# Spreading the latent norm factor of an MLA layer over the partitions: four transposes in place of a DRAM write and read

## The chip, the core and the metric

The kernel runs on one core of one Trainium2 chip. The metric is the device time of one execution in microseconds, as the median over runs. A core has a matrix engine (TensorE, PE in the profile; PEld is its weight load), a vector engine (VectorE, DVE), a scalar engine (ScalarE, ACT), a general engine (GpSimd, POOL) and a sync engine (SyncE, SP), which here issues the DMA transfers. Each engine works through its own queue in order and waits on semaphores for the others. TensorE writes to the accumulator memory PSUM; the working memory is SBUF, with 128 partitions.

## What is computed

A two-layer encoder trunk over 1024 positions of width 1024, batch 1, in float32. Layer 0 is differential attention. Layer 1 is multi-head latent attention, and the change lies at its start:

```python
def _rmsnorm(x, g):
    xf = x.astype(jnp.float32)
    y = xf * lax.rsqrt(jnp.mean(xf * xf, axis=-1, keepdims=True) + RMS_EPS)
    return (y * g.astype(jnp.float32)).astype(x.dtype)

def _mla(h, positions, w_in, q_a_norm_g, w_q_b, kv_a_norm_g, w_kv_b, w_out):
    proj = h @ w_in
    q_a, c_kv, k_pe, z = jnp.split(proj, [384, 640, 704], axis=-1)
    q = (_rmsnorm(q_a, q_a_norm_g) @ w_q_b).reshape(b, s, 8, 192)
    ...
    kv = (_rmsnorm(c_kv, kv_a_norm_g) @ w_kv_b).reshape(b, s, 8, 256)
    k_nope, v = kv[..., :128], kv[..., 128:]
    ...
    return o @ w_out
```

The two latents are the query latent (384 wide) and the key/value latent (256 wide). Each position of a latent is divided by its root mean square over the latent's width and multiplied by a gain per column.

## The kernel before

The kernel keeps activations transposed: partitions hold columns, the free dimension holds positions. Positions come in two halves of 512. Every float32 product is made of three matmuls on a high and a low part of each operand (`mm3`, lines 186 to 188). A high part is a rounding copy on ACT, the low part a subtraction on DVE or GpSimd.

The instructions of each engine are put in order by a planner that uses costs of its own, so the order on the chip isn't always that of the code; only instructions marked with `in_turn`, `issue_after` or `keep_in_program_order` are tied down.

Layer 1 begins with the rotary part of the key, the first gate tiles, and then the latents. `lora` (lines 1397 to 1447) returns the consumer for one latent. The key/value latent has n = 2 tiles of 128 columns for each half, the query latent n = 3. For each tile `put` copies the accumulator to SBUF (L1404) and squares it on ACT (L1408, L1411); DVE adds the squares up (L1412). When the last tile of a half is there, a list called `norms` takes over. `run_norms` (L1373) is called at fixed places of the code, and at each it runs what stands in the list at that moment, which may append the next step. The steps are:

- `norm` (L1419): four small matmuls with a column of ones (L1422) sum the squares over the partitions. The result is a 128x4 tile: position 128 j + p of the half is at partition p, column j. DVE takes the mean and adds epsilon (L1424), GpSimd raises to the power -0.5 (L173), which gives y. Then `bcast_rows` (lines 409 to 415) spreads y: a DMA writes it to DRAM (L412), and a second one reads it back into all 128 partitions as a 128x512 tile (L414). In that tile the position order is p, then j, so the scale reads it through a view with a stride of four elements.
- `scale` (L1428): DVE multiplies a latent tile by the gain of its partition and by the spread factor (L1430), once for each of the n tiles. With n = 3 the three follow in one step; with n = 2 the second is put back on the list.
- `split` (L1439): ACT makes the high part (L1442), DVE the low part (L1443).

Around the key/value norm TensorE makes the gate products of three head pairs (`z_pair`, lines 1527 to 1554), each of seven products of twelve matmuls, with `run_norms` called after some of them. Their weights are combined on DVE (L1489 to L1494) and split by ACT (L234) and GpSimd (L235).

Around the query norm TensorE makes the value tiles: `v1_tile` (L1565), six matmuls into an accumulator, evicted by an ACT copy and a DVE subtraction (L366) and stored to DRAM (L368). The eight tiles of the first column half run with pieces of a stream of products between them:

```python
    stream1.step(QA_V)
    for tt in range(NT):
        v1_tile(tt, 0, p4)
        run_norms()
        if tt < V_IN:
            stream1.step(32 // V_IN)
```

The first 48 steps of the stream are the query latent. After the loop come value tiles of the second column half with four or six steps between (`V1_AT`): two value tiles, the key product of head 0 (L1634, L1635), three value tiles, that of head 1, then the products of the normed query latent (`cq`). Accumulators of all these come from one rotation of five PSUM banks (tag `acc`); a product can start when the one five before it has been evicted. Two further banks have the tag `tr`, for the sums of the norm and for transposes.

Of the kernel before, what the change touches and what calls it, by code (L numbers as in the profile page):

```python
# [11 lines left out]
F32 = mybir.dt.float32  # L12
# [4 lines left out]
ALU = mybir.AluOpType  # L17
# [4 lines left out]
P = 128  # L22
# [4 lines left out]
HF = 512  # L27
# [59 lines left out]
def f32v(ap):  # L87
    return ap.bitcast(F32)
# [3 lines left out]
def trunk(ctx: ExitStack, tc: tile.TileContext, A, out):  # L92
    nc = tc.nc
    SP, PE, V, S, G = nc.sync, nc.tensor, nc.vector, nc.scalar, nc.gpsimd

    def pool(stack, name, bufs=1, side="left", space=None):
        kw = dict(name=name, bufs=bufs, reuse_waits="tile")
        if space is not None:
            kw["space"] = space
            if space == DRAM:  # L100
                kw.pop("reuse_waits")
        else:
            kw["side"] = side
        return stack.enter_context(tc.tile_pool(**kw))
# [19 lines left out]
    def bank(tag, name, shape=None):  # L124
        nonlocal turn
        if tag == "acc":
            turn += 1
            if (turn - 1) % (2 + NB.get("accx", 0)) < 2:
                return psa.tile([P, HF], F32, name=name, tag="acc", bufs=2)
            tag = "accx"  # L130
        return ps.tile(shape or [P, HF], F32, name=name, tag=tag, bufs=NB[tag])
# [12 lines left out]
    ident = const.tile([P, P], F32, name="ident")  # L144
# [9 lines left out]
    def part(name):  # L154
        lo, n = VEC[name]
        return vec[:, lo : lo + n]
# [13 lines left out]
    def rsqrt(w, n):  # L170

        y = sm.tile([P, n], F32, name="rq_y")
        G.tensor_tensor(out=y, in0=w, in1=mhalf[:, :n], op=ALU.pow)  # L173
        return y
# [234 lines left out]
    def bcast_rows(sp, y, tag, bufs):  # L409

        d_ = dr.tile([HF], F32, name="bc_d", tag="bcd", bufs=4)
        SP.dma_start(d_.rearrange("(p t) -> p t", p=P), y)  # L412
        b = sp.tile([P, HF], F32, name="bc_s", tag=tag, bufs=bufs)
        SP.dma_start(b, d_[None, :].to_broadcast([P, HF]))  # L414
        return b, b.rearrange("p (q t) -> p t q", t=4)

    def t3(ap_):
        return ap_.rearrange("p (t q) -> p t q", t=4)
# [100 lines left out]
    wp = pool(stW, "wp0", side="right")  # L519
# [789 lines left out]
    wp = pool(stw, "wp1", side="right")  # L1309
# [4 lines left out]
    def rpt(name, dt=F32):  # L1314
        return wp.tile([P, HF], dt, name=name, tag="rp", bufs=6)
# [55 lines left out]
    norms = []  # L1371
# [25 lines left out]
    def lora(n, dst, gvec, width, raw, part, lag):  # L1397

        craw = [[None, None] for _ in range(n)]
        sums = [None, None]  # L1400

        def put(i, half, acc):
            t = raw()
            S.copy(t, acc)  # L1404
            craw[i][half] = t
            if i == 0:
                sums[half] = pv1.tile([P, HF], F32, name="csum", tag="csum", bufs=2)
                S.activation(sums[half], acc, AF.Square)  # L1408
            else:
                s2 = rpt("csq")  # L1410
                S.activation(s2, acc, AF.Square)  # L1411
                V.tensor_add(sums[half], sums[half], s2)  # L1412
            if i == n - 1:
                f = lambda: norm(half)
                for _ in range(lag):
                    f = lambda f=f: norms.append(f)
                norms.append(f)

        def norm(half):  # L1419
            pt = bank("tr", "cps", [P, 4, P])  # L1420
            for j in range(4):
                PE.matmul(pt[:, 0, j : j + 1], sums[half][:, j * P : (j + 1) * P], ones[:, 0:1], start=True, stop=True)  # L1422
            wv = sm.tile([P, 4], F32, name="c_w")
            V.tensor_scalar(wv, pt[:, 0, 0:4], 1.0 / width, EPS, op0=ALU.mult, op1=ALU.add)  # L1424
            y = rsqrt(wv, 4)
            _, rb = bcast_rows(wp, y, "rp", 6)

            def scale(i=0):  # L1428
                t = craw[i][half]
                tc.keep_in_program_order(V.scalar_tensor_tensor(  # L1430
                    out=t3(t), in0=t3(t), scalar=gvec[:, i : i + 1], in1=rb, op0=ALU.mult, op1=ALU.mult))
                if i + 1 < n:
                    if n == 2:
                        norms.append(lambda: scale(i + 1))
                    else:
                        scale(i + 1)
                norms.append(lambda: split(i))

            def split(i):  # L1439
                t = craw[i][half]  # L1440
                dst[i][half] = hi, lo = part(), part()
                S.copy(hi, t)  # L1442
                V.tensor_sub(lo, t, f32v(hi))  # L1443

            norms.append(scale)

        return put

# [489 lines left out]
```

## Time and profile before

| What | Value |
|---|---|
| median of 3 runs | 1443.95 us (1442.47 to 1446.05) |
| the profiled execution | 1442.89 us |
| its span, first to last instruction | 1441.0 us |
| mean granted TensorE clock | 0.994 |
| key/value latent norm, first sums to last scale | 853 to 877 us of the span |
| query latent norm, first sums to last split | 946 to 973 us of the span |
| scales of the latents (L1430) | 10, 1107 to 1143 ns each |

A row of the timeline gives the start in us, the duration in us, the engine, the line, the operation, the tiles written and read, their shapes, how many instructions are merged, and in brackets the idle time of the engine just before and what ended it. A row of the groups gives the busy time, the mean of one in ns, and the idle time before them with its releasers. In the window table the granted clock is 1.00 at full speed.

### The profile page before, as it was taken

How to read it: one execution, taken by the hardware profiler on the slowest of the kernel's cores; microseconds unless marked ns; L12 is line 12 of the kernel's file. 1: busy time of each engine (PE TensorE's matmuls, PEld its weight loads, DVE VectorE, ACT ScalarE, POOL GpSimd, SP SyncE). 2: the span in 40 equal slices, each digit the busy share in tenths (PEclk: the TensorE clock that was granted, in tenths of full speed). 3: DMA queues.
4: the chain of work that ended last, by engine and by line, in shares of the span. 5: the costliest groups of instructions: out<-in, count | busy, mean ns of one | idle time of the engine just before them, and what ended most of it. 6: DMA issues, size and time to landing. Idle time of an engine off the chain costs nothing. (4 is left out here: it accounts for less than half of the span.)

```text
span 1441.0 us, 20737 instructions
## 1 busy us (share of the span) xinstructions
PE 1399.7 (97%) x7462; PEld 1168.1 (81%) x7462; DVE 906.0 (63%) x1366; ACT 740.3 (51%) x1314; POOL 602.8 (42%) x483
## 2 busy tenths in 40 slices
PE   9998999999999999998999999989999999999997
PEld 7776788888888887887878787868888888888886
DVE  7755787767777767677445867254666555555355
ACT  6622366666565655566343644335554554545442
POOL 4415164656464646463462335413141321412562
PEclk9999999999999999999999999999999999999999
DMA  9876823233332323336663132565344432336663
GB/s 342 263 224 198 261 65 98 83 107 83 95 98 87 96 88 88 89 95 234 227 200 126 56 108 82 154 175 162 119 117 126 126 99 75 102 101 214 217 207 140
DMA packets 129625, 202.70 MB, mean 141 GB/s; under 512 B 18417, under 2 KB 55409, under 8 KB 129522
## 3 DMA queue, kind: packets, MB, share of 16 engines
q1 hardware_dynamic: 129522, 201.37, 45.0%
q8 instruction: 59, 0.97, 0.3%
q14 instruction: 44, 0.36, 0.1%
HBM read 132.16 MB, written 45.56 MB: 123 GB/s over the span
## 5 line engine op out<-in xcount | busy, mean ns | idle before, releaser
L389 ACT CAST pth<-tr 128x512 fp32r<-128x512 f32 x256 | 150.2, 587 | 278.9 <-PE tr L387 276.1
L404 DVE TENSOR_REDUCE nm<-s 128x1 f32<-128x1024 f32 x192 | 233.7, 1218 | 77.3 <-PE s L873 68.4
L390 DVE TENSOR_TENSOR ptl<-tr,pth 128x512 fp32r<-128x512 f32 x256 | 175.9, 687 | 138.1 <-ACT pth L389 137.4
L235 POOL TENSOR_TENSOR wl<-wraw,wh 128x512 fp32r<-128x512 f32 (+2 forms) x82 | 101.6, 1241 | 240.5 <-ACT wh L234 206.4
L387 PE MATMUL tr<-ident,e 128*128 128x128 f32 x1024 | 154.6, 273 | 4.4 <-DVE ptl L390 4.0
L406 ACT ACTIVATE e<-s,nm 128x1024 f32<-128x1024 f32 x128 | 143.5, 1121 | 28.6 <-DVE nm L404 28.1
L387 PEld LDWEIGHTS tr<-ident,e 128*128 128x128 f32 x1024 | 120.9, 140 | 45.9 <-DVE ptl L390 22.0
L186 PE MATMUL acc<-h0h,wh 128*128 128x512 f32 x360 | 150.5, 418 | 1.8 <-DVE v_hl L366 1.7
L186 PE MATMUL pv<-pth,vt 128*128 128x256 f32 x512 | 147.2, 288 | 0.0
L187 PE MATMUL pv<-ptl,vt 128*128 128x256 f32 x512 | 146.0, 285 | 0.0
L188 PE MATMUL pv<-pth,vt 128*128 128x256 f32 x512 | 144.6, 282 | 0.0
L188 PE MATMUL acc<-h0h,wl 128*128 128x512 f32 x360 | 142.4, 396 | 0.1
L187 PE MATMUL acc<-h0l,wh 128*128 128x512 f32 x360 | 141.3, 393 | 0.0
L1117 POOL TENSOR_TENSOR wol<-wor,woh 128x512 fp32r<-128x512 f32 x64 | 84.7, 1343 | 85.2 <-ACT woh L1116 79.7
L186 PEld LDWEIGHTS pv<-pth,vt 128*128 128x128 f32 x512 | 97.2, 190 | 3.4 <-ACT pth L389 0.8
L187 PEld LDWEIGHTS pv<-ptl,vt 128*128 128x128 f32 x512 | 97.4, 190 | 2.9
L188 PEld LDWEIGHTS pv<-pth,vt 128*128 128x128 f32 x512 | 97.6, 191 | 0.1
L873 PE MATMUL s<-ks,qa 128*128 128x512 f32 x256 | 82.7, 403 | 3.5 <-DVE e L881 2.7
L336 POOL TENSOR_TENSOR rp_sw<-rp_sw,sinT 128x512 f32<-128x512 f32 x42 | 55.4, 1318 | 70.3 <-DMA rp_sw<-rp_raw 66.3
L331 POOL TENSOR_TENSOR rp_r<-rp_raw,cosT 128x512 f32<-128x512 f32 x38 | 49.7, 1307 | 81.0 <-ACT rp_raw L326 49.9
L881 DVE SCALAR_TENSOR_TENSOR e<-s,z,e 128x1024 f32<-128x1024 f32 x64 | 82.1, 1283 | 2.1
L873 PE MATMUL s<-ks,qb 128*128 128x512 f32 x256 | 81.1, 396 | 0.7 <-DMA qb<-qb 0.7
(621 smaller groups left out, 3358.0 us busy)
## 6 DMA issues: line engine op xcount, KB each, us to landing
ada<-in_ada_ss SPq DMA_DIRECT2D x32, 512.0 KB, 6.2
wraw<-in_w_s SPq DMA_DIRECT2D x64, 256.0 KB, 2.8
vS<-v_hl SPq DMA_DIRECT2D x32, 512.0 KB, 4.8
vt<-vS SPq DMA_DIRECT2D x32, 512.0 KB, 4.6
wor<-in_w_out SPq DMA_DIRECT2D x64, 256.0 KB, 3.5
rp_sw<-rp_raw SPq DMA_DIRECT2D x168, 64.0 KB, 2.0
bc_s<-bc_d SPq DMA_DIRECT2D x34, 256.0 KB, 4.1
oS<-bc_s SPq DMA_DIRECT2D x30, 256.0 KB, 2.8
```

Of the source, the lines that this page charges most:

```text
L186: PE.matmul(psum, ah, bh, start=first, stop=False)
L187: PE.matmul(psum, ah, bl, start=False, stop=False)
L188: return PE.matmul(psum, al, bh, start=False, stop=last).ins
L235: sub = (lo_on or (V if pair_of else G)).tensor_sub(l_[:, :n], raw[:, :n], f32v(h_[:, :n]))
L387: PE.transpose(tr[:, j, :], p[:, kt * P : (kt + 1) * P], ident)
L389: mk["S"] = S.copy(pth[kh][:, :, dst], tr).ins
L390: mk["V"] = V.tensor_sub(ptl[kh][:, :, dst], tr, f32v(pth[kh][:, :, dst])).ins
L404: mk["V"] = V.reduce_max(nm, s_ps, axis=AX.X, negate=True).ins
L406: mk["S"] = S.activation(e, s_ps, AF.Exp, bias=nm, scale=1.0, accum_out=zs).ins
L873: PE.matmul(s_ps[:, kc * HF : (kc + 1) * HF], src[:, c, ql], KS[h][kc][:, c, :], start=fst, stop=not fst)
L881: combined.append(V.scalar_tensor_tensor(out=e0, in0=e1, scalar=z1[:, 0:1], in1=e0, op0=ALU.mult, op1=ALU.add).ins)
L1117: in_turn(G.tensor_sub(lo, raw, f32v(hi)))
```

## The change

In `norm`, the call of `bcast_rows` goes. A tile `rb` of 128x512 is taken from the same rotation of six (tag `rp`). A new step `spread`, put on the list where `scale` stood, makes four transposes: the input of transpose j is column j of y repeated 128 times, so its result holds y of the 128 positions of block j in every partition. The four fill one PSUM bank of the tag `tr`; ACT copies it to `rb`; then `spread` calls `scale`. The positions in `rb` are in the latent's own order, so the scale reads it without a stride. This holds for both latents and both halves: four sets of four transposes and four copies, in place of four writes and four reads. Other users of `bcast_rows` keep it.

```diff
@@ -1423,12 +1423,19 @@
             wv = sm.tile([P, 4], F32, name="c_w")
             V.tensor_scalar(wv, pt[:, 0, 0:4], 1.0 / width, EPS, op0=ALU.mult, op1=ALU.add)
             y = rsqrt(wv, 4)
-            _, rb = bcast_rows(wp, y, "rp", 6)
+            rb = wp.tile([P, HF], F32, name="rb", tag="rp", bufs=6)
+
+            def spread():
+                tr = bank("tr", "rbp", [P, 4, P])
+                for j in range(4):
+                    PE.transpose(tr[:, j, :], y[:, j : j + 1].to_broadcast([P, P]), ident)
+                S.copy(t3(rb), tr)
+                scale()
 
             def scale(i=0):
                 t = craw[i][half]
                 tc.keep_in_program_order(V.scalar_tensor_tensor(
-                    out=t3(t), in0=t3(t), scalar=gvec[:, i : i + 1], in1=rb, op0=ALU.mult, op1=ALU.mult))
+                    out=t, in0=t, scalar=gvec[:, i : i + 1], in1=rb, op0=ALU.mult, op1=ALU.mult))
                 if i + 1 < n:
                     if n == 2:
                         norms.append(lambda: scale(i + 1))
@@ -1442,7 +1449,7 @@
                 S.copy(hi, t)
                 V.tensor_sub(lo, t, f32v(hi))
 
-            norms.append(scale)
+            norms.append(spread)
 
         return put
```

## The prediction

> **What bounds the kernel now.** I read the page's busy table first.
>
> ```profile
> span 1441.0 us, 20737 instructions
> ...
> PE 1399.7 (97%) x7462; PEld 1168.1 (81%) x7462; DVE 906.0 (63%) x1366; ACT 740.3 (51%) x1314; POOL 602.8 (42%) x483
> ```
>
> TensorE is busy for 97% of the span, so a wait in another engine counts only where it leaves a hole in TensorE's row. I therefore read the stretch windows over the two places where the latent norms run, and kept those with a hole; the last row is the rest of layer 1 up to the final projection. Columns: stretch, length, busy time and instructions of PE, PEld, DVE, ACT, POOL, then granted clock, DMA share, GB/s.
>
> ```profile
> 950.00:957.40 7.40, 7.40 (x35) 6.12 (x33) 1.74 (x4) 1.76 (x3) 0.80 (x1) 1.00 0.94 230
> 957.40:963.00 5.60, 3.52 (x16) 2.48 (x15) 5.46 (x7) 2.34 (x5) 0.23 (x1) 1.00 0.85 163
> 963.00:968.40 5.40, 1.32 (x7) 0.75 (x5) 5.35 (x7) 2.73 (x7) 1.08 (x1) 0.83 0.84 319
> 968.40:973.30 4.90, 4.90 (x12) 3.84 (x13) 3.65 (x7) 2.15 (x5) 0.00 (x0) 0.50 0.73 210
> ...
> 985.00:1390.00 405.00, 402.87 (x2382) 344.06 (x2381) 222.26 (x317) 205.27 (x372) 133.15 (x103) 1.00 0.44 136
> ```
>
> From 957.40 to 968.40 TensorE works 4.84 of 11 us while DVE works 10.81. Just before, DVE was idle for 5.66 of 7.40 us. In the fourth row TensorE is busy but at half its clock. From 985 to 1390 it is idle for 2.13 of 405 us, so time won at 970 should reach the end. The timeline names the cause.
>
> ```profile
> 948.53 0.33 SPq L412 DMA_DIRECT2D bc_d<-rq_y  x1
> 950.99 0.98 SPq L414 DMA_DIRECT2D bc_s<-bc_d  x1
> 953.00 0.69 DVE L366 TENSOR_TENSOR v_hl<-vps,v_hl 128x512 fp32r<-128x512 f32 x1 [0.67 <-ACT v_hl L366]
> 957.36 3.21 DVE L1430 SCALAR_TENSOR_TENSOR cqr<-cqr,vec,bc_s 128x512 f32<-128x512 f32 x3 [3.67 <-DMA bc_s<-bc_d]
> 958.53 0.39 PE L187 MATMUL vps<-wvl,ck 128*128 128x512 f32 x1
> 958.76 0.39 PE L188 MATMUL vps<-wvh,ck 128*128 128x512 f32 x1
> 960.47 0.70 DVE L1635 TENSOR_TENSOR kn_l<-acc,kn_h 128x512 fp32r<-128x512 f32 x1
> 961.23 0.50 PE L186 MATMUL vps<-wvh,ck 128*128 128x512 f32 x1 [2.08 <-DVE kn_l L1635]
> 963.92 0.40 PE L188 MATMUL acc<-ck,wl 128*128 128x512 f32 x1
> 964.55 3.18 DVE L1430 SCALAR_TENSOR_TENSOR cqr<-cqr,vec,bc_s 128x512 f32<-128x512 f32 x3
> 967.66 1.27 DVE L366 TENSOR_TENSOR v_hl<-vps,v_hl 128x512 fp32r<-128x512 f32 x2
> 968.39 0.80 PE L186 MATMUL vps<-wvh,ck 128*128 128x512 f32 x1 [4.08 <-DVE v_hl L366]
> 973.54 0.40 PE L186 MATMUL acc<-cq,wh 128*128 128x512 f32 x1
> ```
>
> The factor leaves for DRAM at 948.53 and the spread copy lets DVE go only at 957.36: 8.8 us. Then three scales run back to back with the low-half subtractions of finished accumulators behind them, and later three more. TensorE runs out of accumulators twice. Matmuls start 0.23 us apart (958.53, 958.76), so the first hole costs 961.23 - 958.76 - 0.23 = **2.24 us** and the second 968.39 - 963.92 - 0.23 = **4.24 us**. After it the twelve matmuls of the half-clock row take 973.54 - 968.39 = 5.15 us where 12 x 0.23 = 2.76 would do: **2.39 us**. That is 8.87 us in the query norm.
>
> The half clock follows the 4.08 us wait, while the row after the 2.08 us wait shows 1.00. The Trainium skill ("TensorE: Matmul & The Clock Gate", Part 1) states that the gate falls to half after an idle window of about 3.4 us. The trace agrees: 4.08 us dropped it, 2.08 did not.
>
> The key/value norm, some 90 us earlier, has a smaller hole of the same family.
>
> ```profile
> 863.35 1.14 DVE L1430 SCALAR_TENSOR_TENSOR craw<-craw,vec,bc_s 128x512 f32<-128x512 f32 x1 [1.72 <-DMA bc_s<-bc_d]
> ...
> 875.58 1.12 DVE L1430 SCALAR_TENSOR_TENSOR craw<-craw,vec,bc_s 128x512 f32<-128x512 f32 x1
> 876.73 0.62 ACT L1442 CAST ck<-craw 128x512 fp32r<-128x512 f32 x1 [3.26 <-DVE craw L1430]
> 877.26 0.61 ACT L234 CAST wh<-zs 128x512 fp32r<-128x512 f32 x1
> ...
> 877.12 0.39 PE L188 MATMUL zacc<-t3h,wl 128*128 128x512 f32 x1
> 877.92 0.50 PE L186 MATMUL zacc<-t1h,wh 128*128 128x512 f32 x1 [0.41 <-ACT wh L234]
> 878.26 0.39 PE L187 MATMUL zacc<-t1l,wh 128*128 128x512 f32 x1
> 879.28 0.50 PE L188 MATMUL zacc<-t1h,wl 128*128 128x512 f32 x1 [0.63 <-POOL wl L235]
> ```
>
> The last scale ends late, the cast of its result holds ACT's queue for 3.26 us, and the weight cast behind it reaches TensorE late: (0.80 - 0.23) + (1.02 - 0.23) = **1.36 us**. In all 10.2 us could come back.
>
> **The change, part by part.**
>
> ```profile
> 761.95 0.60 PE L499 MATMUL trh<-ident,xfull 128*128 128x128 f32 x4
> 762.30 0.48 PE L186 MATMUL oacc<-woh,ot_h 128*128 128x512 f32 x1
> 762.62 0.39 PE L187 MATMUL oacc<-wol,ot_h 128*128 128x512 f32 x1
> ```
> ```profile
> L389 ACT CAST pth<-tr 128x512 fp32r<-128x512 f32 x256 | 150.2, 587 | 278.9 <-PE tr L387 276.1
> ...
> L387 PE MATMUL tr<-ident,e 128*128 128x128 f32 x1024 | 154.6, 273 | 4.4 <-DVE ptl L390 4.0
> ```
> ```profile
> L1430 DVE SCALAR_TENSOR_TENSOR cqr<-cqr,vec,bc_s 128x512 f32<-128x512 f32 x6 | 6.4, 1123 | 3.7 <-DMA bc_s<-bc_d 3.7
> ...
> L1504 DVE SCALAR_TENSOR_TENSOR zu<-zth,zu 128x512 f32<-128x512 f32 x6 | 5.1, 869 | 0.7 <-ACT zth L1503 0.7
> ```
> ```profile
> 879.38 0.69 DVE L1504 SCALAR_TENSOR_TENSOR z<-zth,z 128x512 f32<-128x512 f32 x1 [0.70 <-ACT zth L1503]
> ```
>
> *Added on TensorE.* Four sets of four 128x128 float transposes. The nearest row is a set between long matmuls: from 761.95 to 762.62 there are the four and one matmul, so a set takes 0.67 - 0.23 = 0.44 us. Four sets: **+1.76 us**, on the bounding engine, with nothing to hide them. Here each set reads a repeated column instead of a full block; no row shows that, and I take it at the same price. The bounds are 0.35 us (the next matmul starts at 762.30) and, if nothing overlapped, 4 x 0.273 = 1.09 us for a set: 1.4 to 4.4 us in all, and the quoted set lies near the low end.
>
> The Trainium skill ("TensorE: Matmul & The Clock Gate", Part 4) gives about 275 ns for one transpose in one kernel's context; added up, sixteen would cost 4.4 us by it, as an estimate, which eats most of the gain. The trace has the same length for one (273 ns), but its four make room for the next matmul in 0.35 us, so the lengths do not add.
>
> *Added on ACT.* Four evictions of 128x512 from PSUM at 0.59 us, 2.3 us in all. ACT is busy for 1.76 of 7.40 us from 950 on, so they have cover; without it the split casts queued behind would slip by 0.59 each.
>
> *Changed on DVE.* Ten scales at 1.12 us read the factor at a stride of four; now it lies in order. Same operation, shape and types without the stride: 0.69 with GpSimd quiet, 0.87 on average with it busy. In the query norm GpSimd works 0.23 to 1.08 us per stretch, so I take 0.69 and win 0.43 each: 2.6 us of DVE there, 1.0 to 1.7 in the other norm. DVE is not the bound, so this counts only through the holes.
>
> *Removed on SP.* Four 2 KB writes and four 256 KB reads, with SP standing at each read until the write landed. Behind them stand the stores of the value tiles and the z weight loads. None of the holes is put down to such a load, so I book nothing; those loads can only come earlier.
>
> *The start moves.* The scales of the first query half need y (948.53), the transposes and one eviction: 0.44 + 0.2 + 0.59 on top gives about 950 instead of 957.36. From there DVE owes, until the second key tile at the end of the jam: 6 scales and 6 subtractions for the split, 12 x 0.69 = 8.3 us, and eleven evictions of value and key tiles, 11 x 0.69 = 7.6 us. That is 15.9 us. TensorE makes those eleven tiles in 11 x 6 x 0.23 = 15.2 us, plus about 1.9 for the second sums and one set, and has five accumulators, nearly 7 us of slack. So DVE about keeps pace, where before it started 7 us behind. A bunch of three scales and three casts' subtractions (4.1 us) can still come ahead of an eviction that is due; I leave **1.0 us** of the 8.87 in place. No wait near 4 us means no half clock.
>
> *The new wait.* TensorE's queue is in order, so a transpose whose y is late holds every matmul behind it.
>
> ```profile
> 948.57 0.95 PE L1422 MATMUL cps<-ones,csum 128*128 128x1 f32 x8
> 949.55 0.16 DVE L1424 TENSOR_SCALAR c_w<-cps 128x4 f32<-128x4 f32 x1 [1.53 <-PE cps L1422]
> 949.79 1.01 POOL L173 TENSOR_TENSOR rq_y<-c_w,mhalf 128x4 f32<-128x4 f32 x1 [1.29 <-DVE c_w L1424]
> ...
> 855.37 1.01 POOL L173 TENSOR_TENSOR rq_y<-c_w,mhalf 128x4 f32<-128x4 f32 x1
> ```
>
> From the end of the sums (949.52) to y (950.80) is 1.28 us. In the code a value tile, 6 x 0.23 = 1.38 us, lies between a sum and its transposes, so the two nearly meet: y of the first half left at 948.53, and the sums that now follow its transposes started at 948.57. I take 0.25 us for each query half: **+0.5 us**. In the other norm a product of twelve matmuls, 2.8 us, lies between, and y of its first half (856.38) is there first: no wait. The bounds are 0 and 1.28 for each of four sets.
>
> *The sum.* Query norm 8.87 - 1.0 = 7.87 back; of the other norm's 1.36 half, 0.68, since its scales start some 4 us earlier and are shorter, but the weight cast behind them is ordered anew; less 1.76 and 0.5. That is 6.3 us. The profiled execution took 1442.89 us (span 1441.0 and 1.9 around it), 1.06 below the median of 1443.95, so it would be 1436.6, and the median **1437.7 us**.
>
> **The rivals.** *Half the jam stays.* The order of DVE's queue is made by a planner; it put the first scales after the subtraction at 953.00 although they stand earlier in the code. If it again groups scales ahead of evictions, or leaves them where they were, so that the change starts nothing earlier, only part returns. With half of 8.87 left, 4.43 for 1.0, the gain is 6.3 - 3.4 = 2.9: 1441.0. For it: DVE has next to no spare time in that stretch. Against: the input is there 7 us earlier, when DVE has 5.66 us free.
>
> *Transposes at full price.* A repeated column might keep the four of a set from overlapping: 16 x 0.273 = 4.4 us for 1.76, gain 3.7: 1440.2. The Trainium skill's rule in the page and part named above comes to the same if its lengths are added. The quoted set speaks against it.
>
> *The wait moves into TensorE, and it gets slower.* If the sums, the factor and the transposes of a set follow each other without a tile between, each set waits 1.28 us, and in the second query half the 128x4 operation may stand behind three scales, 2.07 us more, 3.35 together. It decides once that wait comes near 4 us, because the half clock (2.39 us) comes back. Price: 4 x 1.28 + 2.07 + 2.39 + 1.76 = 11.3 us. If the holes were then wholly filled it would still lose 1.1; if only the first hole and half the small one return, 2.9 us, it loses 8.4. The middle is 4.8: 1448.8. For it: the in-order queue and DVE's crowding. Against: a tile lies between in the code.
>
> **How the numbers follow.** A difference of 0.3%, 4.3 us, is about what a measurement of this kernel can tell from none: the runs before lie within 3.6. I give the forecast 0.60, half a jam 0.22, the full-price transposes 0.04, the slower case 0.14. The forecast's own range goes from all 10.2 back without waits, less 1.76 (8.4 won), to 4.4 won: 1435.5 to 1439.6, and 1.3 lower for the scatter of a median. The range, 1434.2 to 1444.5, goes on over the full-price transposes and the half jam, up to where nothing is won; it leaves out the slower case and little else. Faster 0.60, same 0.26, slower 0.14.
>
> **What would show it.** Right: no bc_d or bc_s issue between 843 and 980, the first query scale at about 950 and near 0.69 us, TensorE's holes from 957 to 969 down to about 1 us with the clock at 1.00, about 0.44 us for each set of transposes, and key products of the query latents starting some 6 us earlier. Wrong: a wait of TensorE for rq_y over 1 us, an eviction still waiting behind three scales, a half-clock stretch, or new holes after 985 that give it back.

## The result and the profile after

The changed kernel takes **1433.97 us** (median of 6 runs, 1432.43 to 1439.56); the kernel before, run again beside it, 1443.28 (6 runs). The ratio is **0.9942, 95% interval 0.9929 to 0.9956**: 8.4 us faster by the ratio, 6.4 to 10.2 by its interval; the two medians lie 9.3 apart. The profiled execution took 1434.23 us, its span 8.6 us less than before.

The busy table of the changed kernel:

```profile
span 1432.4 us, 20749 instructions
...
PE 1399.6 (98%) x7478; PEld 1169.8 (82%) x7478; DVE 903.7 (63%) x1366; ACT 743.4 (52%) x1318; POOL 602.7 (42%) x483
```

TensorE has 16 instructions more and is busy for the same time. The 8.6 us are holes and slow matmuls that are gone. Where they went is read by cutting both traces at the same TensorE instructions: the first sum of squares of the key/value latent (K), the first of the query latent (Q), the first product of the query latent (cq), the first scores matmul that reads kn_l (s0), the last cast of kn_h (kn7), and the end. The stretch windows between the first of these marks, before:

```profile
853.40:946.27 92.87, 91.83 (x407) 74.76 (x406) 43.58 (x60) 32.62 (x58) 40.85 (x31) 1.00 0.37 115
946.27:973.54 27.27, 21.11 (x89) 16.75 (x88) 18.35 (x26) 10.32 (x21) 3.59 (x4) 0.87 0.77 207
```

and after:

```profile
852.73:944.76 92.03, 92.03 (x415) 75.77 (x414) 41.60 (x60) 34.37 (x60) 40.15 (x31) 1.00 0.35 110
944.76:964.45 19.69, 19.52 (x98) 15.84 (x97) 16.49 (x27) 11.41 (x22) 3.29 (x4) 1.00 0.78 223
```

K to Q, the stretch of the key/value norm, is 0.84 us shorter although eight transposes more lie in it, and TensorE is busy from end to end. Q to cq, the query norm, is **7.58 us** shorter; TensorE is busy for 19.52 of 19.69 us and the granted clock is 1.00 where it was 0.87. The rest of the difference is 0.67 ahead of K, where both kernels are the same, and 0.5 lost behind cq.

The timeline of the changed kernel over the query norm, in rows that answer to those of the prediction:

```profile
945.99 1.01 POOL L173 TENSOR_TENSOR rq_y<-c_w,mhalf 128x4 f32<-128x4 f32 x1 [0.97 <-DVE c_w L1424]
946.82 0.40 PE L188 MATMUL vps<-wvh,ck 128*128 128x512 f32 x1
947.04 0.41 PEld L1431 LDWEIGHTS rbp<-ident,rq_y 128*128 128x128 f32 x4 [0.26 <-POOL rq_y L173]
947.06 0.64 PE L1431 MATMUL rbp<-ident,rq_y 128*128 128x128 f32 x4
947.53 0.95 PE L1422 MATMUL cps<-ones,csum 128*128 128x1 f32 x8
947.74 0.59 ACT L1432 COPY rb<-rbp 128x512 f32<-128x512 f32 x1
949.21 2.07 DVE L1437 SCALAR_TENSOR_TENSOR cqr<-cqr,vec,rb 128x512 f32<-128x512 f32 x3
949.59 0.40 PE L188 MATMUL vps<-wvh,ck 128*128 128x512 f32 x1
949.82 0.41 PEld L1431 LDWEIGHTS rbp<-ident,rq_y 128*128 128x128 f32 x4 [0.28 <-POOL rq_y L173]
950.56 0.40 PE L187 MATMUL vps<-wvl,ck 128*128 128x512 f32 x1
951.19 0.68 DVE L366 TENSOR_TENSOR v_hl<-vps,v_hl 128x512 fp32r<-128x512 f32 x1
954.39 2.07 DVE L1437 SCALAR_TENSOR_TENSOR cqr<-cqr,vec,rb 128x512 f32<-128x512 f32 x3
959.45 0.39 PE L187 MATMUL vps<-wvl,ck 128*128 128x512 f32 x1
960.01 0.50 PE L186 MATMUL vps<-wvh,ck 128*128 128x512 f32 x1 [0.17 <-DVE v_hl L366]
```

The reader is to see four things. From the factor (947.00) to the first scale (949.21) it takes 2.2 us, where the trip through DRAM had taken 8.8. Three scales take 2.07 us, 0.69 each. The eviction behind the first three, at 951.19, is in time for TensorE; the one behind them before, at 960.47, ended a wait of TensorE of 2.08 us. And one wait of 0.17 us is left of the two of 2.08 and 4.08.

### The profile page after: what moved, and what is told of

The parts are those of the page before. It is cut to its first block, busy times and chain, and to the rows that moved or that the text cites. A ratio compares the mean times of both kernels' runs of the same rounds, so it can differ in the third digit from the quotient of the medians.

```text
span 1432.4 us, 20749 instructions
## 1 busy us (share of the span) xinstructions
PE 1399.6 (98%) x7478; PEld 1169.8 (82%) x7478; DVE 903.7 (63%) x1366; ACT 743.4 (52%) x1318; POOL 602.7 (42%) x483
## 4 chain that ended last, share of the span: by engine, by line
PE 84%; DMA 4%; DVE 4%; ACT 2%; POOL 2%; issue 2%; SPq 1%; POOLq 0%; ACTq 0%; DVEq 0%
PE s L1702 10%; PE acc L186 9%; PE acc L188 9%; PE acc L187 9%; PE tr L387 7%; PE s L873 7%; PE pv L187 4%; PE pv L188 4%; PE pv L186 4%; PE oacc L187 3%; PE oacc L188 3%; PE oacc L186 3%; PE zacc L186 1%; PE zacc L188 1%; PE zacc L187 1%
```

## The experiments

**The theory.** DVE starts the scales of the query latent some 7 us earlier, while it has room, and each is 0.43 us shorter, so TensorE is no longer held for a free accumulator. The start counts most. **The rivals**: the shorter scales alone do it; the removed DMAs do it; the key/value norm does it; or the planner's order elsewhere does it.

The kernels ran in three groups beside the kernel before, whose medians there were 1441.00 (19 runs), 1441.42 (27) and 1441.21 (17). The intervals are from one profiled execution each, in us.

| kernel | median (runs) | ratio to before, 95% | K to Q | Q to cq | cq to s0 | s0 to kn7 |
|---|---|---|---|---|---|---|
| before | 1443.28 (6) | 1 | 92.87 | 27.27 | 10.4 | 289.8 |
| after | 1433.97 (6) | 0.9942 [0.9929, 0.9956] | 92.03 | 19.69 | 10.3 | 290.4 |
| after_again | 1433.57 (5) | 0.9949 [0.9935, 0.9963] | 92.02 | 19.67 | 10.3 | 290.6 |
| q_only | 1434.14 (7) | 0.9955 [0.9941, 0.9969] | 92.79 | 19.66 | 10.3 | 289.9 |
| kv_only | 1440.93 (10) | 1.0002 [0.9991, 1.0013] | 92.03 | 27.05 | 10.3 | 290.4 |
| strided | 1435.26 (7) | 0.9968 [0.9950, 0.9985] | 92.03 | 22.00 | 10.3 | 290.4 |
| late2 | 1437.94 (10) | 0.9973 [0.9962, 0.9984] | 92.03 | 20.50 | 10.3 | 292.3 |
| late5 | 1437.61 (10) | 0.9973 [0.9963, 0.9982] | 92.02 | 20.78 | 12.8 | 289.8 |
| dma_back | 1438.91 (10) | 0.9988 [0.9977, 0.9999] | 92.02 | 19.70 | 10.3 | 294.3 |
| dma_hold | 1436.11 (5) | 0.9965 [0.9953, 0.9977] | 92.01 | 19.65 | 10.3 | 290.9 |
| tiny_dma | 1434.27 (6) | 0.9958 [0.9945, 0.9970] | 92.03 | 19.66 | 10.3 | 289.8 |
| triple | 1440.45 (12) | 0.9994 [0.9982, 1.0005] | 94.26 | 21.45 | 10.3 | 291.8 |
| psum_direct | 1434.28 (5) | 0.9954 [0.9942, 0.9966] | 92.03 | 19.67 | 10.3 | 290.1 |

dram_contig (1457.12 us, 4 runs, ratio 1.0117 [1.0096, 1.0139]) is told below. From kn7 on, all kernels of the table take 167.2 to 168.1 us. The start of K, which no edit touches, lies anywhere from 849.9 to 854.5, so the total of one profile says less than its intervals.

**One latent at a time.** In q_only the transposes serve the query latent alone and the key/value latent keeps its trip through DRAM; kv_only is the reverse, with n == 2 in the two places.

```diff
+            if n == 3:
+                rb, v3 = wp.tile([P, HF], F32, name="rb", tag="rp", bufs=6), lambda ap_: ap_
+            else:
+                rb, v3 = bcast_rows(wp, y, "rp", 6)[1], t3
...
-            norms.append(spread)
+            norms.append(spread if n == 3 else scale)
```

> The transposes for the query latent alone; the key/value latent keeps its DRAM write and read. Theory (the gain comes from the start of the scales in the query norm, where DVE idled and then jammed): nearly the whole gain stays, 7 to 8 us of the 8.4 (1435 to 1436.5), TensorE's holes of 2.08 and 4.08 us and the half clock are gone, and the hole of 1.36 us in the key/value norm is still there. Rival (four round trips fewer on the DMA queue, each worth the same): about half, 1439.

> The transposes for the key/value latent alone. Theory: 0 to 1.5 us won (1442 to 1443.3), the two holes and the half clock of the query norm stay as before. Rival of equal shares per round trip: about 4 us won, 1439.

The waits of TensorE from 840 us on, q_only:

```profile
PE zacc L188 <- POOL wl L235: 0.6, 1, 0.6
PE zacc L186 <- ACT wh L234: 0.4, 1, 0.4
...
PE vps L186 <- DVE v_hl L366: 0.2, 1, 0.2
```

and kv_only:

```profile
PE vps L186 <- DVE kn_l L1645: 4.1, 1, 4.1
...
PE vps L186 <- DVE v_hl L366: 1.7, 1, 1.7
```

Each half of the change removes the holes of its own norm and leaves the other's. The query half alone gives the whole time within what can be measured. The key/value half shows its 0.84 us in K to Q, and its total can't be told from none. The planner's order elsewhere earns nothing: from cq to s0 the kernel before and the changed one take the same within 0.1 us, and from s0 to kn7 the changed one takes 0.6 us more.

**Early, but with the strided read.** The copy writes the old position order, and the scales read it with the stride of four as before. TensorE's order is that of the changed kernel, instruction by instruction.

```diff
-                S.copy(t3(rb), tr)
+                S.copy(rb.rearrange("p (q t) -> p t q", t=4), tr)
...
+                    out=t3(t), in0=t3(t), scalar=gvec[:, i : i + 1], in1=rb.rearrange("p (q t) -> p t q", t=4), op0=ALU.mult, op1=ALU.mult))
```

> As the changed kernel, but the eviction lays the factor down in the old order (position p, then block), so the scales read it with the stride of four again: early start, scales at 1.12 us. Theory (the early start counts): 6 query scales x 0.38 = 2.3 us more DVE work, which the five accumulators take up in part, so 0.5 to 2 us are given back: 1434.5 to 1436. Rival (the stride made the jam): 5 us or more given back, 1439 or later, with TensorE holes of 2 us and more.

```profile
946.46 1.08 ACT L1432 COPY rb<-rbp 128x512 f32<-128x512 f32 x1
947.93 3.23 DVE L1437 SCALAR_TENSOR_TENSOR cqr<-cqr,vec,rb 128x512 f32<-128x512 f32 x3
954.32 3.23 DVE L1437 SCALAR_TENSOR_TENSOR cqr<-cqr,vec,rb 128x512 f32<-128x512 f32 x3
958.20 0.50 PE L186 MATMUL vps<-wvh,ck 128*128 128x512 f32 x1 [0.79 <-DVE kn_l L1642]
961.04 0.50 PE L186 MATMUL vps<-wvh,ck 128*128 128x512 f32 x1 [1.42 <-DVE v_hl L366]
```

In this timeline of strided three scales take 3.23 us, as long as before, and start early. Of the 7.58 us in the query norm 5.27 are kept (27.27 to 22.00); 2.3 are given back, a little more than the 0.5 to 2 that were expected of the total. So the early factor is worth some 70% of it, the short scales and the shorter copy (0.59 us for 1.08) the rest.

**Short scales, but through DRAM.** The factor is written to DRAM in position order, so that the scales read without a stride, and read back as before.

```diff
-            _, rb = bcast_rows(wp, y, "rp", 6)
+            d_ = dr.tile([HF], F32, name="bc_d", tag="bcd", bufs=4)
+            SP.dma_start(d_.rearrange("(t p) -> p t", p=P), y)
+            rb = wp.tile([P, HF], F32, name="bc_s", tag="rp", bufs=6)
+            SP.dma_start(rb, d_[None, :].to_broadcast([P, HF]))
...
```

> The kernel before, but the DRAM write puts the factor into position order, so the read brings an ordered tile and the scales read it without a stride: late start, scales at 0.74 us. The write is in pieces of 4 bytes instead of 16 and may land later. Theory (the late start counts): the jam stays; each three scales take 2.1 instead of 3.2 us, so each hole shrinks by about 1.1 us, and the half clock goes if the second falls under some 3.4 us: 2 to 5 us won, 1438.5 to 1441.3. Rival (the stride made the jam): 7 us won, 1436.

The expectation missed what the new write costs. In the timeline of dram_contig:

```profile
952.81 0.38 SPq L1427 DMA_DIRECT2D bc_d<-rq_y  x1
962.73 0.33 SPq L1429 DMA_DIRECT2D bc_s<-bc_d  x1
968.21 2.08 DVE L1433 SCALAR_TENSOR_TENSOR cqr<-cqr,vec,bc_s 128x512 f32<-128x512 f32 x3 [10.23 <-DMA bc_s<-bc_d]
970.94 0.79 PE L186 MATMUL vps<-wvh,ck 128*128 128x512 f32 x1 [7.52 <-DVE kn_l L1638]
```

and its waits of TensorE from 840 us on:

```profile
PE vps L186 <- DVE v_hl L366: 10.3, 1, 10.3
PE vps L186 <- DVE kn_l L1638: 7.5, 1, 7.5
PE zacc L186 <- ACT wh L234: 2.6, 1, 2.6
```

Each partition's four values now go to four places, in pieces of 4 bytes, and the read could be issued only 9.9 us after the write; before, with pieces of 16 bytes, it was 2.5 (948.53 to 950.99). The scales are as short as they can be (2.08 for three), DVE waits 10.23 us before them, and TensorE waits 7.5 and 10.3 us in the query norm. So the run doesn't separate the start from the length as it was meant to. It shows the other end of the same: with a factor that comes still later the short scales don't help, K to Q takes 98.09 us and Q to cq 40.43, and the kernel 1457.12 - 1441.00 = 16.1 us more. The 2 to 5 us that were expected to be won were missed.

**Early factor, late scales.** The changed kernel with the step `scale` of the query latent put back on the list, two rounds (late2, below) or five (late5, with 5 in place of 2). after_again is the changed kernel itself, run beside them.

```diff
-                scale()
+                f = scale
+                for _ in range(2 if n == 3 else 0):
+                    f = lambda f=f: norms.append(f)
+                f()
```

> The changed kernel once more, beside the runs of this call: both theories, 7 to 9 us under the kernel before (ratio 0.994 to 0.995).

> As the changed kernel, but the query scales are written two value tiles later in the code, so they follow in DVE's queue the evictions that they followed before, with the factor long there. Theory (the wait of DVE for the factor made the jam, not the order): scales start about 3 us later than in the changed kernel and 4 before the old start; 0 to 2 us given back. Rival (the order of DVE's queue, scales ahead of key evictions, made the jam): 5 us or more given back.

> As the changed kernel, but the query scales are written five value tiles later, behind the key evictions, so they start about when they did before (958), unstrided and with no DMA. Theory (the late start counts): 12 operations of 0.69 to 0.75 us and five evictions, some 12 us of DVE work, then stand before the first query product, which TensorE reaches at 964.5: TensorE waits for the query latent, 3 to 6 us given back. Rival (stride or DMA made the jam): the whole gain stays, within 1 us.

late5 gives back what was expected, 4.0 us by the medians, and its waits of TensorE show the other side of the balance:

```profile
PE acc L186 <- ACT cq L1452: 1.8, 2, 1.4
...
PE acc L187 <- DVE cq L1453: 0.6, 2, 0.4
```

With the scales behind the key tiles no accumulator is late any more, but the products of the query latent wait for cq: 1.1 us more up to cq and 2.5 more up to s0. The first scales of late5:

```profile
961.69 2.07 DVE L1440 SCALAR_TENSOR_TENSOR cqr<-cqr,vec,rb 128x512 f32<-128x512 f32 x3
```

They start 15.2 us behind Q (946.50 here), later than the 11.1 of the kernel before (946.27 to 957.36), and still 4.0 of the 7.6 us up to s0 stay won. So a late start, with the factor there and the evictions ahead of the scales, costs about half of the gain. What the trace of the kernel before has on top is that DVE stood 3.67 us for a factor that wasn't there, with the evictions behind the scales in its queue, and that the scales were longer.

late2 was expected to give back 0 to 2 us and missed: it gives back 4.4 by the medians. Its first scales start 8.4 us behind Q, 3.9 later than in the changed kernel, and that costs only 0.8 in the norm; 1.7 more go at the first attention tile, and the other 1.9 stand in no interval of its profile. The first attention tile leads to the next question.

**The DMAs put back.** dma_back is the changed kernel with the four writes and four broadcast reads issued as well, into a DRAM tile that nothing reads.

```diff
+            d_ = dr.tile([HF], F32, name="bc_d", tag="bcd", bufs=4)
+            SP.dma_start(d_.rearrange("(p t) -> p t", p=P), y)
+            SP.dma_start(dr.tile([P, HF], F32, name="dmy", tag="dmy", bufs=4), d_[None, :].to_broadcast([P, HF]))
```

> As the changed kernel, with the four writes of the factor to DRAM and four broadcast reads issued as before, the reads into a DRAM tile that nobody uses. Theory: nothing in the path waits for them; 0 to 1 us given back. Rival (SP's queue, which stood at each read, or the traffic held up other transfers): 3 us or more given back.

This missed: 5.3 us are gone by the medians, 3.7 of them between s0 and kn7 in the profiled execution. But the norms are as fast as in the changed kernel (K to Q 92.02, Q to cq 19.70), and that loss stands at the first attention tile. The window of dma_back and its timeline there:

```profile
984.40:988.50 4.10, 4.10 (x16) 3.26 (x14) 0.69 (x1) 1.11 (x3) 0.00 (x0) 0.58 0.92 275
```
```profile
981.28 0.39 PE L187 MATMUL acc<-cq,wh 128*128 128x512 f32 x1
983.96 0.65 PE L387 MATMUL tr<-ident,e 128*128 128x128 f32 x4 [2.29 <-ACT e L406]
985.73 1.06 PE L1705 MATMUL s<-kn_h,qn_l 128*128 128x512 f32 x2
```

The changed kernel run again, at the same place:

```profile
985.83 0.40 PE L186 MATMUL acc<-cq,wh 128*128 128x512 f32 x1
986.06 0.60 PE L387 MATMUL tr<-ident,e 128*128 128x128 f32 x4
986.98 0.62 PE L1702 MATMUL s<-kn_l,qn_h 128*128 128x512 f32 x2
```

TensorE's order in dma_back differs from that of the changed kernel in one stretch only, of some 30 us, which begins among the scores of the first attention tile. The transposes of the first e come after 8 products of the query latent and not after 13, e isn't there, TensorE waits 2.29 us and then runs at a granted clock of 0.58. late2 and triple have the same order from the first scores on, and the same wait (2.19 and 2.30 us) at a clock of 1.00; their s0 to kn7 is 1.9 and 1.4 us longer than the 290.4 of the changed kernel. The half clock, 4.10 us at 0.58, is worth about 1.7 more in dma_back. So two more kernels were made. dma_hold adds two writes, two broadcast reads and two 256 KB stores, chosen so that the order of all four compute engines stays that of the changed kernel. tiny_dma adds one store of 16 bytes, after which the planner makes a third order.

```diff
+            if n == 2:
+                d_ = dr.tile([HF], F32, name="bc_d", tag="bcd", bufs=4)
+                SP.dma_start(d_.rearrange("(p t) -> p t", p=P), y)
+                SP.dma_start(dr.tile([P, HF], F32, name="dmy", tag="dmy", bufs=4), d_[None, :].to_broadcast([P, HF]))
...
+                if n == 3:
+                    SP.dma_start(dr.tile([P, HF], F32, name="dmy3", tag="dmy3", bufs=4), rb)
```
```diff
+            if n == 3 and half == 1:
+                SP.dma_start(dr.tile([1, 4], F32, name="dmy", tag="dmy", bufs=4), y[0:1, 0:4])
```

> The after kernel with unused transfers: in the key/value norm a write of the factor in 4-byte pieces and a 256 KB broadcast read for each half, in the query norm a 256 KB store of the spread factor for each half. The order of TensorE, DVE, ACT and GpSimd is that of the after kernel, everywhere. Theory (the transfers cost nothing; dma_back lost its 5 us because its TensorE starts the first attention tile in another order): within 1 us of the after kernel's 1434, the interval from the first scores matmul to the last cast of kn_h at 290 to 291 us, and no wait of 2 us at the first transposes of e. Rival (the transfers themselves cost time, by SP's waits or the memory): 1438 to 1439, as dma_back.

> The after kernel with one unused store of 16 bytes in the second query half. TensorE's order is that of the after kernel up to the first attention tile, and differs from there on. Theory (only the order counts): the norm stage stays as it was, 19.7 us from the second sums to the first product of the query latent, and whatever the total does shows in the interval from the first scores matmul to the last cast of kn_h, between 1 us shorter and 4 us longer than 290.5. Rival (the order is indifferent, transfers cost by their size): all intervals within 0.5 us and the total within 0.7 us of the after kernel's.

By the edit the pieces of dma_hold's writes are of 16 bytes, as in the kernel before, and not of 4 as its expectation says. The waits of TensorE in dma_hold:

```profile
PE tr L387 <- DVE ptl L390: 1.7, 2, 1.4
PE s L1708 <- DMA qpa<-qpa: 1.1, 1, 1.1
PE vps L186 <- DVE v_hl L366: 0.2, 1, 0.2
```

With the order held there is no wait for e, and s0 to kn7 is 290.9. The total is 1.8 us above that of psum_direct, which ran in the same group, so more than the 1 us of the theory and well under the 5 of dma_back, though the intervals of the two ratios overlap; a wait of 1.1 us for a load of qpa (0.5 in psum_direct) and 0.6 us behind kn7 are what its trace has for it. tiny_dma loses nothing, by total or by interval: another order need not cost, and as nothing was lost, the run can't tell its theory from its rival. What follows: the order of the first attention tile, which late2 and triple share without the transfers, accounts for some 2 of dma_back's 5.3 us, and the half clock behind the same wait for about 1.7. How much of the rest is the transfers' own, up to about 2 us, stays open.

**The price of the transposes.** triple issues every set three times.

```diff
-                for j in range(4):
+                for j in (0, 1, 2, 3) * 3:
```

> Each set of four transposes is issued three times into the same bank, eight sets more in all. Theory (0.44 us a set, in line with the quoted set): 1.8 us more in each norm, 93.8 us from the first key/value sums to the first query sums and 21.5 from there to the first product of the query latent: 3.5 us. Rival (the four of a set do not overlap, 1.09 us a set): 4.4 us more in each norm, 8.7 in all. TensorE's order at the first attention tile is that of dma_back; if its loss sits in that order, some 3.5 us come on top, so about 1441 by the theory and 1446 by the rival.

K to Q grows by 2.2 us and Q to cq by 1.8 against the changed kernel: 4.0 for eight sets more, at most 0.50 a set. The timeline of triple has the first twelve:

```profile
853.73 0.39 PE L188 MATMUL zacc<-t3h,wl 128*128 128x512 f32 x1
853.96 1.47 PE L1431 MATMUL rbp<-ident,rq_y 128*128 128x128 f32 x12
855.27 0.95 PE L1422 MATMUL cps<-ones,csum 128*128 128x1 f32 x8
```

855.27 - 853.96 = 1.31 us for three sets is 0.44 a set and 0.11 for a transpose. The full price is refuted; some 0.5 of the 2.2 us in K to Q isn't in these rows and stays unplaced. The total, 1440.45 where about 1441 was expected and 6.2 us above psum_direct's, has 4.0 of these; by subtraction some 2 are left for the order at the first attention tile, which is dma_back's, and the profile shows 1.7 there (291.8 for 290.1).

**Without the copy.** In psum_direct the scale reads the bank of the transposes itself.

```diff
...
-                S.copy(t3(rb), tr)
+                rb.append(tr.rearrange("p t q -> p (t q)"))
...
```

> The scale reads the factor straight from the PSUM bank of the transposes, without the ACT copy. TensorE's order is that of the after kernel. Theory: the scales start 0.6 us earlier, of the hole of 0.33 us in the query norm at most that much returns, so the same within 1 us, and the key/value norm gains nothing. Rival: the two banks of the tag are held through the scales, two microseconds longer, so a later sum or transpose waits for a bank on TensorE, 1 to 3 us slower.

The theory holds: 1434.28 us, the intervals as in the changed kernel, no wait for a bank. The scales take 0.74 us each from PSUM. A copy less on ACT is worth nothing here, and no experiment found a kernel that beats the changed one.

## Why the prediction came out as it did

The direction and the mechanism were right, and the gain was larger than forecast: 8.4 us by the ratio and 8.6 by the spans, against 6.3. The median lies 0.2 us below the low end of the range. By its own steps:

- *The early start and the short scale*: right. About 950 and 0.69 us were predicted; 949.21 and 0.69 were found in the query norm. In the key/value norm, with GpSimd busy, the four took 1.06, 1.17, 0.74 and 0.74: 0.8 us less than before, where 1.0 to 1.7 were predicted. Part of what the early start was worth, by late5, is that DVE no longer stands waiting for the factor with evictions behind it.
- *The residual of the jam, 1.0 us*: mis-sized. The one hole left costs 960.01 - 959.45 - 0.23 = 0.33. The stretch as a whole says the same: 7.58 us returned and 0.99 for the two sets (worked out below) make 8.57 of 8.87, so 0.3 remained.
- *The transposes at 0.44 a set*: right, by triple and by the rows. In the key/value norm:

```profile
856.41 0.60 PE L1431 MATMUL rbp<-ident,rq_y 128*128 128x128 f32 x4
856.84 0.95 PE L1422 MATMUL cps<-ones,csum 128*128 128x1 f32 x8
...
860.26 0.39 PE L188 MATMUL zacc<-t1h,wl 128*128 128x512 f32 x1
860.49 0.60 PE L1431 MATMUL rbp<-ident,rq_y 128*128 128x128 f32 x4
861.16 0.40 PE L187 MATMUL zacc<-t4l,wh 128*128 128x512 f32 x1
```

  A set takes 856.84 - 856.41 = 0.43 and 861.16 - 860.49 - 0.23 = 0.44.
- *The wait for y, 0.25 for each query half*: mis-sized. The weight load of the transposes waits 0.26 and 0.28 us, but a matmul is still running beside it. From 946.82 to 947.53 lie one matmul, the wait and a set, 0.71 - 0.23 = 0.48; from 949.59 to 950.56 two matmuls, the wait and a set, 0.97 - 0.46 = 0.51. That is 0.99 for both, of which the waits are about 0.1, not 0.5.
- *Half of the key/value hole*: the most mis-sized term. The forecast for that norm was 0.68 - 0.88 = -0.2; it measured +0.84. The whole 1.36 us came back: ck's casts no longer hold ACT, and the weight casts behind them are in time. Some 0.36 us more than that hole returned, and no row places it.
- *The removed DMAs, booked at nothing*: right for the norms, since dma_back has both at full speed with the transfers put back. Behind them, up to about 2 us stay open.
- *The time won at 970 reaches the end*: it did, but for 0.5 us. That was not assured: with the order that late2, triple and dma_back have at the first attention tile, s0 to kn7 is 1.4 to 3.9 us longer than in the changed kernel (3.9 with the half clock). The prediction named new holes behind 985 as a sign that it is wrong and gave them no price.

In sum 1.1 us of the difference from 6.3 to 8.4 is the query norm (0.7 residual, 0.4 waits for y) and 1.0 the other norm. The three rivals are answered: half the jam would have left 4.4 us of holes in the query norm, and 0.3 is left; the full price is refuted by triple; the sums, the factor and the transposes have a value tile between them, so the wait never grew past 0.28 us.

## What to carry to other kernels

A value that must reach all partitions in the middle of a crowded stage is worth the 0.44 us that four transposes cost the busiest engine, if the trip through DRAM delays work for an engine that has room now and none later, with other due work behind it in that engine's queue; look for the idle time just before the jam. Judge such a change by the intervals between fixed instructions, since an edit as small as a DMA can make a planner reorder a stage that it never touches, and kernels with another order of that stage took up to 3.9 us longer in it here. And when layouts are changed to make a read contiguous, look at who pays: the contiguous read saved 0.4 us a scale, and the 4-byte write that allowed it came 7 us later.

## What the hardware showed beside this

- A write of 512 values from 128 partitions to DRAM in pieces of 4 bytes held the read behind it for 9.9 us; in pieces of 16 bytes, 2.5. From issue to landing the four writes took 8.2 us against 1.4, by the DMA views of dram_contig and of the kernel before from 840 to 1010 us.
- Transposes of a column repeated 128 times run like those of a full block: 0.27 us each, 0.11 apart.
- The prediction read the half clock as following a wait near 4 us, with 2.08 not enough, and the Trainium skill ("TensorE: Matmul & The Clock Gate", Part 1) as agreeing with it, about 3.4 us of idle time. dma_back's profile has a half-clock stretch (0.58) behind a wait of 2.29 us, while late2 and triple, with 2.19 and 2.30, kept 1.00. So the length of the wait alone doesn't decide. The traces hold more. The half clock lasts from 984.96 to 988.37 in dma_back, 3.41 us, and from 966.53 to 973.36 in the kernel before, twice that. Take the 3.41 us just before it: TensorE was busy for 1.13 of them in dma_back (981.54 to 984.96, with the whole wait inside) and for 1.19 in the kernel before (963.12 to 966.53). Steps of 3.41 us counted on from the half-clock stretch that triple and late2 each have near 140 us have a boundary inside the wait of 2.3 or 2.2, and their least busy steps keep more: 1.68 (983.33 to 986.74) and 1.81 (983.74 to 987.15). So around these waits the work within one such step goes with the clock of the next. No exact bound comes out (in strided, at 566.48 to 569.90, 1.72 of 3.42 us went before a half clock), and that it decides was not tested.
- A copy from PSUM on ACT takes 1.08 us when it writes with a stride of four elements and 0.59 in order, 1.8 times; a scale on DVE that reads the factor with that stride takes 1.08 for 0.69 (strided and the changed kernel), 1.6 times.
